# A difference made by GpSimd or by ScalarE: every second block of the modulated prompt rows in a streaming encoder layer

## The chip, the cores and the metric

The kernel runs on one core of a Trainium2 chip. A core has five engines that run their own instruction streams and wait for each other on semaphores: TensorE (PE: matrix products and transposes, results into PSUM), VectorE (DVE), ScalarE (ACT), GpSimd (POOL) and SyncE (SP, which issues most of the DMAs here). The on-chip memories are SBUF and PSUM; PSUM is used in eight banks of 128 x 512 fp32.

The metric is the device time of one execution in microseconds (us). Times below are medians of several executions; one further execution was recorded by the hardware profiler, and all lines of a profile or trace in this document come from such recorded executions.

## What is computed

The reference is one layer of a streaming encoder for a prompt of 2048 rows and for 8 running streams of 16 rows each, with rows of 1024 numbers. Its first step is a normalisation with a modulation per sequence:

```python
def adaln_modulate(x, c, norm_g, w_ada, b_ada):
    mod = c @ w_ada + b_ada
    shift, scale, gate = jnp.split(mod, 3, axis=-1)
    h = rms_norm(x, norm_g) * (1.0 + scale[:, None, :]) + shift[:, None, :]
    return h, gate[:, None, :]
```

From `h` follow ten projections (`h @ w_in`), rotary embedding of some of them, a differential attention with 4 heads, a stick-breaking attention with 8 heads, gates, a merge of the two branches, an output projection, a residual and a last normalisation. Keys and values are outputs too. All inputs and outputs are fp32.

## The kernel before

**Numbers.** TensorE is fed with fp16 pairs: a value v is kept as an upper half hi = fp16(v) and a lower half lo = fp16(v - hi), and a product of two such values takes three fp16 products (hi hi, hi lo, lo hi).

**Tiles.** The prompt has 16 tiles of 128 rows; the 8 streams together are a 17th tile, the sample tile. The rows are taken in five groups (`GROUPS`): groups 0 to 3 of 512 prompt rows (four tiles) and group 4, the sample tile.

**Phases.** In the first phase the conditioning vectors are multiplied with `w_ada` (`modulation`, six parts; parts 4 and 5, for the gate, run at the end of the phase), the rows are normalised (`normed`: squares on ScalarE at L298, a reciprocal root on VectorE at L258 to L269, then the scaling of the rows, for groups 1 to 3 by GpSimd at L1169, four instructions of 128 x 1024 for a group), and turned and modulated (`modulated`). The result h, as fp16 halves, goes to DRAM (`hT_d`), and the tiles in hand also feed projections directly. In the second phase eight units follow (unit = one pair of heads of one of the two attentions); each unit projects its 17 tiles (L467, gate products at L543), computes scores, weights and outputs. In the third phase the branches are merged and the output projection is made.

**`modulated(g)`, the place of the change.** One group is made in eight pieces k = 0 to 7, one for each 128 of the 1024 columns. A piece for a prompt group does this:

1. TensorE transposes four 128 x 128 fp32 blocks into one PSUM bank (L1233). Even k use a bank of the kind "s" (three of them), odd k a bank of the kind "o" (two of them).
2. ScalarE makes the upper half: hi = fp16(scale * p + shift), from PSUM into `hp` (L1239).
3. ScalarE makes hi - shift, fp32, into the scratch tile `tmp` (L1241); `minus_b` holds the negative shift, one number for each partition. `tmp` has two buffers, which `modulation` also uses (`ms`, L1144).
4. VectorE makes the lower half: lo = fp16(scale * p - tmp), from PSUM and `tmp` into `hp` (L1242). After it the bank and the scratch tile are free.
5. After the last piece SP stores the group (L1251).

The sample group (group 4) takes other lines (L1245 to L1249).

**Order.** Pieces of `modulated(g)`, of `normed(g + 1)` (or of the gate's modulation, for g = 3) and of the first projections of unit 0 (`take(position(...))`) are interleaved when the program is written down. The order on each engine is then set by a planner, which runs the program on a simulated time line (`schedule_with_timeline_sim=True`); instructions marked by `keep_in_program_order` keep theirs. On the chip each engine works through its stream in the planned order. In the profile the planner's order can be seen: upper halves run ahead of the differences of earlier pieces.

**Beside it.** Projections of unit 0 run in the same phase: TensorE's products (L467), ScalarE's scaled copy `pr` (L481), the upper halves of values, queries and keys (L318, L501), VectorE's lower halves of them (L323, L502), GpSimd's rotary embedding (L508, L510, L513) and SP's loads and stores.

Of the kernel before, what the change touches and what calls it, by code (L numbers as in the profile page):

```python
# [21 lines left out]
AF = mybir.ActivationFunctionType  # L22
ALU = mybir.AluOpType
# [101 lines left out]
def layer_kernel(ctx: ExitStack, tc: tile.TileContext, a: dict):  # L125
    nc = tc.nc
    V, S, G, T = nc.vector, nc.scalar, nc.gpsimd, nc.tensor
# [83 lines left out]
    def bank(tag, dt=F32):  # L211
        return ps.tile([P, 512 if dt == F32 else 1024], dt, tag=tag, name=f"ps_{tag}", bufs=BANKS[tag])
# [841 lines left out]
    with tc.tile_pool(name="p0", bufs=1) as p0:  # L1054
# [8 lines left out]
        def hp_tile(dt):  # L1063
            hp = p0.tile([P, 4096], F32, tag="hp", name="hp", bufs=3)
            return hp.bitcast(dt) if dt != F32 else hp
# [125 lines left out]
        def wide(x):  # L1191
# [24 lines left out]
                        scalar1=sh[:, 0:1], scalar2=None, op0=ALU.mult)  # L1216
        minus_b = p0.tile([P, KT], F32, name="minus_b")
        V.tensor_scalar(out=minus_b, in0=ab[:, 1, :, 0], scalar1=-1.0, scalar2=None, op0=ALU.mult)

        def modulated(g):  # L1220

            t0, w = GROUPS[g]
            nt = w // P
            box = {}

            def piece(k):
                if k == 0:
                    box["hp"] = hp = hp_tile(F16)[:, 0 : nt * 2 * D].rearrange("p (i a k n) -> p i a k n", a=2, k=KT, n=P)
                    at_hand.update({t0 // P + i: hp[:, i, :, :, :] for i in range(nt)})
                hp = box["hp"]  # L1230
                pt = bank("so"[k % 2])
                for i in range(nt):
                    T.transpose(pt[:, i * P : (i + 1) * P], xs[g][i][:, k * P : (k + 1) * P], ident)  # L1233
                tmp = p0.tile([P, 512], F32, tag="tmp", name="tmp", bufs=2)
                hi, lo = hp[:, :, 0, k, :], hp[:, :, 1, k, :]
                pv = pt[:, 0:w].rearrange("p (i n) -> p i n", n=P)
                tv = tmp[:, 0:w].rearrange("p (i n) -> p i n", n=P)
                if t0 < SEQ:
                    S.activation(out=hi, in_=pv, func=AF.Identity, scale=ab[:, 0, k, 0:1], bias=ab[:, 1, k, 0:1])  # L1239

                    S.activation(out=tv, in_=hi, func=AF.Identity, bias=minus_b[:, k : k + 1])  # L1241
                    V.scalar_tensor_tensor(out=lo, in0=pv, scalar=ab[:, 0, k, 0:1], in1=tv, op0=ALU.mult, op1=ALU.subtract)  # L1242
                else:
                    tb = tmp[:, 0:w].rearrange("p (b s) -> p b s", b=NB)
                    V.tensor_tensor(out=tb, in0=pt[:, 0:w].rearrange("p (b s) -> p b s", b=NB),  # L1245
                                    in1=ab[:, 0, k, 1:9].unsqueeze(2).to_broadcast([P, NB, NS]), op=ALU.mult)
                    V.tensor_tensor(out=tb, in0=tb, in1=ab[:, 1, k, 1:9].unsqueeze(2).to_broadcast([P, NB, NS]), op=ALU.add)
                    S.copy(out=hi, in_=tv)
                    G.tensor_tensor(out=lo, in0=tv, in1=hi, op=ALU.subtract)  # L1249
                if k == KT - 1:  # L1250
                    load(out=hT_d[g], in_=hp)  # L1251

            return [(1.0, lambda k=k: piece(k)) for k in range(KT)]

        def gates():
# [166 lines left out]
    for n in range(len(steps) + 2):  # L1422
# [19 lines left out]
        if at[0] == len(line) and not spare and not cached:  # L1442
            m = n - len(steps)
            if behind:
                k = -(-len(behind) * LATE_SHARE[m] // sum(LATE_SHARE[m:]))
                pieces += [(1.0, fn) for fn in behind[:k]]
                del behind[:k]
            if m >= -CUTS_AT:
                if cuts is None:
                    cuts = early_work()  # L1450
                k = -(-len(cuts) // (len(steps) + 2 - n))
# [189 lines left out]
```

## Time and profile before

| | us |
|---|---|
| median of 3 runs | 2224.91 |
| lowest and highest of them | 2220.69, 2227.12 |
| the profiled execution, whole time | 2226.87 |
| the profiled execution, span from the first to the last instruction | 2225.0 |

Durations are read from the profiled execution, so they are held against its own time; its whole time is 1.87 us above its span.

How to read the lines: an instruction is given by its line in the kernel, engine, operation, and out<-in by the names of the tiles with the shapes (partitions x elements, type). A group's line has its count, busy us and mean ns of one, and the idle time of the engine just before, with what ended it. A time line gives start, duration, and in brackets the idle time before, with its releaser. PEld are TensorE's weight loads, which overlap its products. A busy time in a stretch is the time in which an instruction of the engine was running; ends of products are modelled, since they are pipelined.

### The profile page before, as it was taken

What the parts mean: (1) busy time and instruction counts of PE and PEld (TensorE: products, weight loads), DVE (VectorE), ACT (ScalarE), POOL (GpSimd) and SP (SyncE); (2) the same over time, 40 slices, a digit from 0 to 9 for tenths busy, and PEclk for the clock granted to TensorE, in tenths of its full rate; (3) what the DMA queues carried; (4) which work ended last, traced back from release to release, by engine and by line L of the source; (5) the groups of instructions that cost most, each with busy time, mean ns of one, the idle gap of its engine ahead of it and who ended that gap; (6) DMA issues with size and microseconds to landing.
All of it is one profiled execution on the core that took longest, in us unless ns stands there. A gap on an engine that the chain in (4) does not pass through costs nothing.

```text
span 2225.0 us, 41210 instructions
## 1 busy us (share of the span) xinstructions
PE 2048.1 (92%) x14472; PEld 1089.3 (49%) x14472; DVE 1743.2 (78%) x3787; ACT 1605.3 (72%) x3212; POOL 719.5 (32%) x620
## 2 busy tenths in 40 slices
PE   3999999999999999999989998999997789899997
PEld 1545555555555455555554544555454344444443
DVE  5668868889886788988678888887689778787864
ACT  3978677788877787978777788876588575666531
POOL 0523024366311444742034365301345312211210
PEclk9999999999999999999999999999999899999999
DMA  9777669799796889979888999876677999889752
GB/s 333 261 246 183 128 151 224 181 221 209 184 266 164 217 199 207 212 192 227 190 207 203 182 237 223 231 171 136 151 165 174 192 280 251 217 250 235 188 155 67
DMA packets 824977, 451.03 MB, mean 203 GB/s; under 512 B 556122, under 2 KB 763274, under 8 KB 824256
## 3 DMA queue, kind: packets, MB, share of 16 engines
q1 hardware_dynamic: 823820, 448.01, 82.6%
q8 instruction: 113, 1.85, 0.4%
q14 instruction: 96, 0.79, 0.1%
q10 hardware_dynamic: 948, 0.39, 0.1%
HBM read 229.87 MB, written 86.02 MB: 142 GB/s over the span
## 4 chain that ended last, share of the span: by engine, by line
PE 27%; DVE 8%; DMA 7%; ACT 5%; issue 3%; POOL 2%; SPq 1%; DVEq 0%; POOLq 0%; ACTq 0%
PE ps_mm L467 7%; PE ps_t L543 6%; PE ps_o L1540 5%; PE ps_mm L1506 3%; DMA wt<-sc_n 2%; PE ps_s L708 1%; DVE sc_n L682 1%; PE ps_s L709 1%; DMA hs<-hT_d 1%; DMA hs<-o_d 1%; DMA dwt<-dsc 1%; ACT sc_p L134 1%; POOL sc_p L688 1%; PE ps_o L769 1%; ACT ps_s L134 1%
## 5 line engine op out<-in xcount | busy, mean ns | idle before, releaser
L688 POOL TENSOR_TENSOR sc_p<-sc_p,sc_n 128x127 f32<-128x127 f32 (+7 forms) x192 | 312.2, 1629 | 665.5 <-DVE sc_n L682 516.0
L467 PEld LDWEIGHTS <-hs 128*128 128x128 f16 x3120 | 293.3, 99 | 326.3 <-DMA hs<-hT_d 11.6
L467 PE MATMUL ps_mm<-wa,hs 128*128 128x512 f16 x1590 | 391.7, 382 | 10.8 <-DMA hs<-hT_d 9.2
L467 PE MATMUL ps_mm<-wb,hs 128*128 128x512 f16 x1530 | 380.1, 382 | 0.0
L682 DVE TENSOR_TENSOR_SCAN sc_n<-ps_s,sc_n,zero_t 128x512 f32<-128x512 f32 x192 | 245.4, 1278 | 30.6 <-ACT ps_s L134 25.1
L543 PE MATMUL ps_t<-wa,hs 128*128 128x512 f16 x1020 | 243.6, 381 | 3.3 <-DVE qst L576 2.3
L543 PEld LDWEIGHTS <-hs 128*128 128x128 f16 x1632 | 154.9, 98 | 186.2 <-DVE qst L576 6.3
L708 PE MATMUL ps_s<-k,qst 128*128 128x512 f16 (+3 forms) x640 | 222.8, 349 | 24.1 <-DVE sc_n L682 20.7
L619 DVE TENSOR_TENSOR sc_n<-sc_p,sc_n 128x128 f16<-128x128 f32 (+7 forms) x192 | 213.6, 1115 | 37.3 <-ACT sc_n L616 36.7
L134 ACT ACTIVATE sc_p<-ps_s,usc 128x512 f32<-128x512 f32 (+3 forms) x320 | 204.7, 640 | 36.0 <-PE ps_s L709 24.3
L709 PE MATMUL ps_s<-k,qst 128*128 128x512 f16 (+3 forms) x640 | 223.1, 349 | 0.0
L616 ACT CAST sc_n<-sc_p 128x128 f16<-128x128 f32 (+7 forms) x192 | 155.6, 811 | 60.6 <-POOL sc_p L688 59.9
L134 ACT ACTIVATE ps_s<-ps_s,usc 128x512 f32<-128x512 f32 (+3 forms) x320 | 197.0, 616 | 0.0
L543 PE MATMUL ps_t<-wb,hs 128*128 128x512 f16 x612 | 151.3, 382 | 7.8 <-DMA hs<-hT_d 4.4
L769 PE MATMUL ps_o<-v,wt 128*128 128x128 f16 x1088 | 134.4, 223 | 25.5 <-DMA wt<-sc_n 25.5
L1540 PE MATMUL ps_o<-wo,wb 128*128 128x512 f16 x624 | 144.8, 388 | 1.7 <-ACT wb L1314 1.7
L602 DVE TENSOR_SCALAR_CACHE_REDUCE sc_p<-ps_s,usc 128x512 f32<-128x512 f32 (+3 forms) x160 | 106.2, 664 | 33.3 <-PE ps_s L709 22.0
L1549 POOL TENSOR_TENSOR x<-m,x 128x512 f32<-128x512 f32 x32 | 47.0, 1468 | 255.4 <-DVE m L1544 161.8
L769 PEld LDWEIGHTS <-wt 128*128 128x128 f16 x1088 | 100.4, 100 | 54.3 <-DMA wt<-sc_n 29.6
L770 PE MATMUL ps_o<-v,wt 128*128 128x64 f16 x1088 | 126.2, 195 | 0.0
L682 DVE TENSOR_TENSOR_SCAN sc_n<-ps_s,zero_t 128x128 f32<-128x128 f32 (+3 forms) x128 | 104.1, 814 | 26.2 <-ACT ps_s L134 26.2
L1506 PEld LDWEIGHTS <-wa 128*128 128x128 f16 x816 | 77.8, 98 | 92.7 <-issue 6.3
(380 smaller groups left out, 4538.5 us busy)
## 6 DMA issues: line engine op xcount, KB each, us to landing
hs<-hT_d SPq DMA_DIRECT2D x132, 512.0 KB, 4.7
g_d<-gt SPq DMA_DIRECT2D x68, 256.0 KB, 4.7
out_dram<-pr SPq DMA_DIRECT2D x204, 64.0 KB, 3.3
o_d<-o SPq DMA_DIRECT2D x136, 64.0 KB, 2.3
wa<-g_d SPq DMA_DIRECT2D x17, 512.0 KB, 4.2
wb<-g_d SPq DMA_DIRECT2D x17, 512.0 KB
hs<-o_d SPq DMA_DIRECT2D x17, 512.0 KB, 4.0
wide<-in_w_ada_dram SPq DMA_DIRECT2D x8, 1024.0 KB, 12.6
```

The source lines that it names most:

```text
L134: i = S.activation(**kw)
L467: T.matmul(box["p"], box["h"][:, hi, k, :], U["w"][k][:, wi, :], start=(n == 0), stop=(n == 3 * KT - 1))
L543: x = T.matmul(box["g"][:, 0:gw], box["h"][:, hi, k, :], U["wg"][k // per][:, k % per, wi, :], start=(j == 0), stop=(j == 3 * KT - 1))
L616: x = S.copy(out=hi, in_=src)
L619: V.tensor_tensor(out=lo, in0=src, in1=hi, op=ALU.subtract)
L682: V.tensor_tensor_scan(out=dst[:, lo : lo + n][:, ::-1], data0=src[:, 0:n][:, ::-1], data1=zero_t[:, 0:1].to_broadcast([P, n]), initial=fi ...
L688: G.tensor_tensor(out=p[:, 0:m], in0=p[:, 0:m], in1=n[:, 1 : m + 1], op=ALU.mult)
L708: T.matmul(p[:, 0:n], qst[:, c, :], kk[:, c, 0:n], start=True, stop=False)
L709: T.matmul(p[:, 0:n], qst[:, 2 + c, :], kk[:, c, 0:n], start=False, stop=not diag)
L769: T.matmul(po[:, c * P : (c + 1) * P], wt[:, wj, :], vt[:, c, :, :], start=first, stop=False)
L1506: T.matmul(pb, st["u"][:, ui * 8 + br * 4 + k, :], wb[br * 4 + k // 2 * 2 + j][:, wi, k % 2, :], start=(n == 0), stop=(n == 11))
L1540: T.matmul(po, st["y"][:, yi * 8 + k, :], wo[j * 4 + k // 2][:, wi, k % 2, :], start=(n == 0), stop=(n == 3 * KT - 1))
```

## The change

For odd k (every second piece of groups 0 to 3) the difference hi - shift is made by a GpSimd instruction with two operations (add the negative shift, add zero), not by ScalarE's activation. Even k, the upper halves, the lower halves and the sample group stay as they are.

```diff
                 if t0 < SEQ:
                     S.activation(out=hi, in_=pv, func=AF.Identity, scale=ab[:, 0, k, 0:1], bias=ab[:, 1, k, 0:1])

-                    S.activation(out=tv, in_=hi, func=AF.Identity, bias=minus_b[:, k : k + 1])
+                    if k % 2:
+                        G.tensor_scalar(out=tv, in0=hi, scalar1=minus_b[:, k : k + 1], scalar2=0.0, op0=ALU.add, op1=ALU.add)
+                    else:
+                        S.activation(out=tv, in_=hi, func=AF.Identity, bias=minus_b[:, k : k + 1])
                     V.scalar_tensor_tensor(out=lo, in0=pv, scalar=ab[:, 0, k, 0:1], in1=tv, op0=ALU.mult, op1=ALU.subtract)
```

`G` is GpSimd, `S` ScalarE and `V` VectorE. The numbers written to `tv` are the same in both forms.

## The prediction

> **What bounds the kernel now.** I read the page's totals first, then the busy times of the stretch in which the changed line runs, then what each engine waited for there, and last the single instructions around those waits. The totals:
>
> ```profile
> span 2225.0 us, 41210 instructions
> PE 2048.1 (92%) x14472; PEld 1089.3 (49%) x14472; DVE 1743.2 (78%) x3787; ACT 1605.3 (72%) x3212; POOL 719.5 (32%) x620
> ```
>
> Over the whole span TensorE is the busiest engine; it is idle for 2225.0 - 2048.1 = 176.9 us. The changed line belongs to one short phase. The groups of ScalarE's instructions (line, operation, shapes, count, busy us, mean ns, idle before) and the busy times by stretch (stretch, length, then PE, PEld, DVE, ACT, POOL, granted clock, DMA) say how short:
>
> ```profile
> L1241 ACT ACTIVATE tmp<-hp,minus_b 128x512 f32<-128x512 f16 x32 | 22.3, 740 | 0.2
> 58.00:84.00 26.00, 21.96 (x132) 13.48 (x131) 18.48 (x50) 25.20 (x47) 17.07 (x20) 0.99 0.69 230
> 84.00:108.00 24.00, 23.42 (x157) 12.78 (x157) 12.44 (x24) 22.97 (x45) 8.49 (x12) 1.00 0.84 285
> 108.00:134.00 26.00, 23.77 (x169) 13.58 (x167) 13.44 (x34) 20.43 (x40) 6.54 (x9) 1.00 0.68 243
> sum 76.00, PE 69.16 PEld 39.83 DVE 44.36 ACT 68.60 POOL 32.10; mean PE 23.05 PEld 13.28 DVE 14.79 ACT 22.87 POOL 10.70
> ```
>
> All 32 instructions of the line lie in these 76 us. ScalarE is busy for 68.60 of them, TensorE for 69.16: two engines are full at once, because the planner fills TensorE with projection products of the first unit (L467) between the transposes. From 58 to 84 ScalarE has 0.80 us left. So relief of ScalarE can shorten this phase only where TensorE really stands still, 76.00 - 69.16 = 6.84 us in all. TensorE's waits there (waiter, released by, us in total, times, longest) name them:
>
> ```profile
> PE ps_s L1147 <- DVE col L307: 1.8, 1, 1.8
> PE ps_mm L467 <- ACT hp L1248: 1.7, 1, 1.7
> PE ps_o L1233 <- DVE hp L1242: 1.1, 1, 1.1
> PE ps_mm L467 <- POOL hp L1249: 1.1, 1, 1.1
> PE ps_mm L467 <- DVE v L323: 0.7, 1, 0.7
> PE ps_mm L1142 <- DVE v L323: 0.4, 1, 0.4
> ```
>
> They add up to 6.8 us. That is the ceiling of a direct gain, 0.31% of the span.
>
> **The change part by part.**
>
> Removed: 16 of the 32 differences leave ScalarE. Half of 22.3 us is 11.2 us busy, 68.60 becomes 57.4 of 76.
>
> Added: 16 GpSimd instructions, fp16 to fp32, 128x512, with two operations. The trace has no such form. The nearest rows are the weight halves of L320 (two operations, 128x512, fp32 to fp16, min/median/max ns) and, for an upper end, a 128x512 addition of two inputs:
>
> ```profile
> L320 POOL TENSOR_SCALAR wb<-wa,sw x4: 692/708/799, 138.5 to 140.6; 128x512 f16<-128x512 f32 x4
> L1549 POOL TENSOR_TENSOR x<-m,x 128x512 f32<-128x512 f32 x32 | 47.0, 1468 | 255.4 <-DVE m L1544 161.8 <-DVE usq L1357 48.8 <-DVE m L1547 27.8
> ```
>
> I take 0.71 us, since L320 has the size, the operation and one tensor input; the ends are 0.69 and 1.47 us. 16 x 0.71 = 11.4 us, and GpSimd goes from 32.10 to 43.5 us of 76 (at 1.47 us to 55.6). An odd block's difference therefore takes as long as before (0.71 against 0.74 us). A GpSimd result reaches a waiting engine quickly, and so does ScalarE's:
>
> ```profile
> 123.28 0.83 POOL L513 TENSOR_TENSOR rot<-rot,r 128x256 f32<-128x256 f32 x1
> 124.14 0.51 ACT L501 ACTIVATE qbuf<-rot,sq 128x256 f16<-128x256 f32 x1 [0.90 <-POOL rot L513]
> ```
>
> The addition ends at 124.11 and ScalarE starts at 124.14: a hop of 0.03 us, and the change adds one such hop to an odd block. I put it at nothing.
>
> Moved: nothing in DMA. The store of a group's h (L1251) is issued from SP after the last lower half as before; only GpSimd's queue has new entries.
>
> What the relief is worth at each wait, one by one. The 1.1 us of L1233 is a transpose of an odd block that waits for an odd bank, hence for VectorE's lower half, hence for the difference:
>
> ```profile
> 63.26 0.76 ACT L1239 ACTIVATE hp<-ps_o,ab 128x512 f16<-128x512 f32 x1
> ...
> 68.14 1.33 ACT L1241 ACTIVATE tmp<-hp,minus_b 128x512 f32<-128x512 f16 x2
> ...
> 68.89 0.75 DVE L1242 SCALAR_TENSOR_TENSOR hp<-ps_o,ab,tmp 128x512 f16<-128x512 f32 x1 [0.18 <-ACT tmp L1241]
> ```
>
> The upper half was there at 64.02, and ScalarE came to the difference only at 68.14. GpSimd can do it near 64, so I count the whole 1.1 us. The 1.8 us is VectorE's copy L1144 (the row names the instruction after it), which stood behind a lower half waiting for its difference:
>
> ```profile
> 120.12 0.75 DVE L1242 SCALAR_TENSOR_TENSOR hp<-ps_s,ab,tmp 128x512 f16<-128x512 f32 x1 [1.51 <-ACT tmp L1241]
> 120.97 0.69 DVE L1144 COPY tmp<-ps_mm 128x512 f32<-128x512 f32 x1
> ```
>
> That block is even (bank s) and keeps ScalarE; it profits only if ScalarE comes to it earlier. The 0.7 us waits for a value half behind ScalarE's full queue. I count half of these two, (1.8 + 0.7) / 2 = 1.25 us. The other three (1.7, 1.1, 0.4) stay: the first two are the sample tile's group, done on other lines, and the last a 0.4 us I leave. **Sum: 1.1 + 1.25 = 2.4 us** gained at the end of the phase, with 0 and 6.8 us as ends. Behind it TensorE stays the bound (379 of each 400 us, rows below), so I let the gain pass to the end.
>
> What VectorE could lose. While GpSimd runs, some VectorE instructions with both inputs in SBUF are stretched, the lower halves are not:
>
> ```profile
> 57.18 0.29 DVE L1247 TENSOR_TENSOR tmp<-tmp,ab 128x128 f32<-128x128 f32 x1
> ...
> 58.33 1.02 DVE L1247 TENSOR_TENSOR tmp<-tmp,ab 128x128 f32<-128x128 f32 x1
> ...
> 80.63 0.74 DVE L1242 SCALAR_TENSOR_TENSOR hp<-ps_s,ab,tmp 128x512 f16<-128x512 f32 x1
> ```
>
> The second L1247 starts inside a run of L1169 on GpSimd and takes 0.73 us more; the L1242 lies inside another such run and takes its usual 0.74. If each new instruction held up one VectorE instruction for its 0.71 us, that is at most 11.4 us, against 76.00 - 44.36 = 31.6 us that VectorE is free there. That cover is why I cost it at nothing; with no cover, a held-up instruction in front of a transpose would cost its 0.7 us. The Trainium skill, page "SBUF — State Buffer", section "Who interferes with whom", gives a rule that speaks against the change: GpSimd and VectorE share one pair of ports as an exclusive lock, taken by VectorE instructions with two SBUF inputs and by its two-port modes. By it the lower half, with one input in PSUM, is free of the lock and the sum stays; the trace agrees with 0.74 us inside the run.
>
> **The rivals.**
>
> ScalarE alone sets the pace (B). For it: 25.20 of 26 us at the start, no gap of note. Then all of TensorE's waits go, and the time falls by 6.8 us. Against it: three of the six waits do not hang on the moved instruction, and TensorE has only those 6.84 us to give. Time: 2218.1. The Trainium skill, "Perfetto Trace Analysis", section "Identifying the Most-Contended Engine", would judge for B: it takes occupancy for ScalarE and calls the busy share of matmuls a bad measure of headroom. The trace speaks against it in this phase: six L467 products follow each other every 0.216 us and leave no holes to close.
>
> ```profile
> 90.41 1.46 PE L467 MATMUL ps_mm<-wa,hp 128*128 128x512 f16 x6
> 91.71 0.28 PE L561 MATMUL ps_t<-id,k 128*128 128x128 f16 x2
> ```
>
> The slower side is GpSimd's queue (C). The differences stand in it behind runs of four L1169:
>
> ```profile
> 67.55 4.42 POOL L1169 TENSOR_SCALAR wide<-wide,rstd 128x1024 f32<-128x1024 f32 x4 [0.53 <-PE ps_mm L467]
> ...
> 78.26 4.42 POOL L1169 TENSOR_SCALAR wide<-wide,rstd 128x1024 f32<-128x1024 f32 x4 [4.09 <-issue]
> ```
>
> A difference caught behind a whole run is up to 4.4 us late. Queued behind the waiting lower half on VectorE are the next block's lower half and the value and key halves (L323), so products and transposes wait too. The slack is small: the next odd block's transposes take the bank some two us after the lower half ends,
>
> ```profile
> 79.96 0.75 DVE L1242 SCALAR_TENSOR_TENSOR hp<-ps_o,ab,tmp 128x512 f16<-128x512 f32 x1 [1.20 <-ACT tmp L1241]
> ...
> 82.86 0.60 PE L1233 MATMUL ps_o<-ident,wide 128*128 128x128 f32 x4
> ```
>
> 82.86 - 80.71 = 2.15 us. C decides when a difference is later than that: 4.4 - 2.15 = 2.3 us for each of the two runs, 4.6 us, and none of the gain: 2224.9 + 4.6 = 2229.5. At 1.47 us an instruction, two more 0.76 us, 2231. Against it: the planner knows both and can put differences between the four.
>
> The plan is drawn anew (D). The order of every engine is set by a simulated time line, and new durations early can shift choices to the end. Three stretches of like work show what layout is worth:
>
> ```profile
> 400.00:800.00 400.00, 382.08 (x2749) 209.71 (x2747) 334.89 (x707) 321.56 (x687) 155.22 (x134) 1.00 0.86 207
> 800.00:1200.00 400.00, 378.67 (x2705) 207.64 (x2703) 329.01 (x694) 316.43 (x673) 153.60 (x131) 0.99 0.88 204
> 1200.00:1600.00 400.00, 376.53 (x2654) 204.51 (x2652) 322.27 (x662) 309.16 (x662) 143.53 (x123) 0.98 0.85 193
> ```
>
> TensorE is idle 17.9, 21.3 and 23.5 us in them, a spread of 2.8. Some 5.2 such stretches follow the phase: 2.8 x the root of 5.2 = 6.4 us with mixed signs, 14.6 with one sign. I take 10 between them: 2212.5 (D down) or 2232.5 (D up). That the change does not do what it says is the 1.47 us end: GpSimd as slow as its two-input form; it goes with C.
>
> **How the numbers follow.** The sum is against the profiled execution: span 2225.0, 2226.87 us with what lies around it, which is 1.96 above the median of 2224.91. The forecast on the span is 2222.6, on the median 2224.9 - 2.4 = 2222.5, own range 2218 to 2225. About 0.3% (6.7 us, so 2218.2 and 2231.6) is what a measurement of this kernel can tell from no change. Chances: forecast 0.43, B 0.10, C 0.13, D down 0.16, D up 0.18. Faster takes D down and half of B, which ends on the bound: 0.21. Slower takes D up and a third of C: 0.22. Within: 0.57. Both signs of D are wanted in the range, with a few us of spread each: 2211 to 2235.
>
> **What would show it.** In the changed profile ScalarE's 58 to 134 us should read near 57 us, L1241 x16, a new GpSimd group x16 near 710 ns, and TensorE's wait for L1242 near 64 to 70 us gone. Idle of TensorE before L1233 released by L1242, with GpSimd's L1169 ahead of it, is C. An unchanged start of the units and another idle sum after 134 us is D. An instruction far from 0.71 us, a phase shorter by more than 6.8 us, or lower halves stretched beside GpSimd would make the prediction wrong.

## The result and the profile after

The changed kernel takes 2241.47 us (median of 6, 2235.26 to 2242.55), the kernel before 2223.28 us (6, 2220.69 to 2230.45): a ratio of 1.0082, 95% interval 1.0065 to 1.0099. It is slower by 18.2 us where 2222.5 was forecast, and beyond the range's end of 2235. In the kernel after, the lines behind L1241 are shifted: **L1242** is GpSimd's difference for odd k, **L1244** ScalarE's for even k, **L1245** the lower half (L1242 before), **L1254** the store of a group (L1251 before), L1251 and L1252 the sample group's. L1233, L1239 and everything ahead of L1241 keep their numbers.

The totals of the kernel after, from the page:

```profile
span 2239.7 us, 41224 instructions
PE 2057.5 (92%) x14472; PEld 1095.9 (49%) x14472; DVE 1753.2 (78%) x3787; ACT 1597.9 (71%) x3196; POOL 745.3 (33%) x636
```

TensorE executes the same 14472 products; by the page its idle time grew from 176.9 to 182.2 us and its busy time by 9.4 us, to which we come back under the clock. The first place to look is the phase. The kernel after, busy times by stretch (columns as in the prediction):

```profile
58.00:84.00 26.00, 17.07 (x85) 8.69 (x84) 19.68 (x48) 17.98 (x33) 22.92 (x23) 0.93 0.47 141
84.00:108.00 24.00, 23.27 (x148) 13.36 (x147) 10.21 (x20) 18.78 (x35) 18.37 (x16) 1.00 0.72 246
108.00:134.00 26.00, 23.32 (x159) 13.15 (x158) 13.40 (x27) 19.48 (x36) 17.52 (x15) 0.93 0.83 314
sum 76.00, PE 63.66 PEld 35.20 DVE 43.29 ACT 56.25 POOL 58.81; mean PE 21.22 PEld 11.73 DVE 14.43 ACT 18.75 POOL 19.60
```

ScalarE fell to 56.25 us (57.4 was worked out; some of the phase's work now lies behind 134 us). GpSimd rose to 58.81, not to 43.5; in the first stretch it is busy for 22.92 of 26 us and TensorE for 17.07, where it had 21.96. The line itself says why. The kernel after, one line's instructions (min/median/max ns, first and last start us):

```profile
L1242 POOL TENSOR_SCALAR tmp<-hp,minus_b x16: 1997/1998/2037, 67.5 to 135.3; 128x512 f32<-128x512 f16 x16
```

**One instruction takes 2.00 us, not 0.71**, and all sixteen do. The stores of h, the same view before and then after:

```profile
L1251 SPq DMA_DIRECT2D hT_d<-hp x5: 320/339/605, 67.1 to 133.3; - x5
```

```profile
L1254 SPq DMA_DIRECT2D hT_d<-hp x5: 319/343/414, 67.5 to 142.7; - x5
```

The last group is stored at 142.7 instead of 133.3: the phase ends 9.4 us later. Its first upper half (L1239) starts at 59.2 us after and at 58.8 before, so 9.0 us of this arise in the phase itself. What TensorE waited for from 58 to 134 us after the change (waiter, releaser, us in total, times, longest):

```profile
PE ps_o L1233 <- DVE hp L1245: 6.1, 2, 4.2
PE ps_s L1233 <- DVE hp L1245: 1.9, 2, 1.1
PE ps_mm L467 <- POOL hp L1252: 1.8, 1, 1.8
PE ps_mm L467 <- ACT hp L1251: 1.7, 1, 1.7
```

Transposes wait 8.0 us for a bank that a lower half has to free; before, 1.1 us. How the longest of these comes about shows in the time line of the kernel after (GpSimd's rows, with those of the other engines that belong to the chain):

```profile
67.55 2.00 POOL L1242 TENSOR_SCALAR tmp<-hp,minus_b 128x512 f32<-128x512 f16 x1
67.89 0.77 ACT L1239 ACTIVATE hp<-ps_o,ab 128x512 f16<-128x512 f32 x1
69.52 4.41 POOL L1169 TENSOR_SCALAR wide<-wide,rstd 128x1024 f32<-128x1024 f32 x4
73.89 0.73 POOL L508 TENSOR_TENSOR rot<-pr,rope 128x256 f32<-128x256 f32 x1
73.96 0.68 DVE L262 TENSOR_SCALAR rstd<-rs_i 128x4 int32<-128x4 int32 x1 [0.99 <-POOL wide L1169]
74.57 0.73 POOL L510 TENSOR_TENSOR r<-pr,rope 128x256 f32<-128x256 f32 x1
75.28 3.97 POOL L1242 TENSOR_SCALAR tmp<-hp,minus_b 128x512 f32<-128x512 f16 x2
78.58 0.16 DVE L269 TENSOR_TENSOR rstd<-rstd,rs_t 128x4 f32<-128x4 f32 x1
78.66 0.75 DVE L1245 SCALAR_TENSOR_TENSOR hp<-ps_o,ab,tmp 128x512 f16<-128x512 f32 x1
79.47 0.66 PE L1233 MATMUL ps_o<-ident,wa 128*128 128x128 f32 x4 [4.16 <-DVE hp L1245]
79.51 0.72 ACT L1244 ACTIVATE tmp<-hp,minus_b 128x512 f32<-128x512 f16 x1 [3.38 <-DVE hp L1245]
```

The upper half of an odd block is there at 68.66. Its difference stands behind the four L1169, L508 and L510, and starts at 75.28; with 2.00 us for itself it ends at 77.28. VectorE reaches the lower half at 78.66, after the reciprocal roots of the next group (L262 to L269), which stood as one block from 73.96. TensorE's transposes then start at 79.47 after 4.16 us of idle time, and ScalarE, which was to be relieved, stands still for 3.38 us behind the same lower half, since `tmp` has only two buffers. In this order the 2.00 us are not the last thing on the path: an instruction of 0.70 us would have ended at 75.98, and the lower half would still have stood behind the roots until 78.58. The longest wait is made by the places in the two streams as well as by the instruction's time.

The wait has an echo on TensorE itself. The kernel after, its products before and behind the wait, and the stretches around it (the last three columns are the granted clock, the DMA share and GB/s):

```profile
72.12 2.75 PE L467 MATMUL ps_mm<-wa,hp 128*128 128x512 f16 x12
...
79.96 4.44 PE L467 MATMUL ps_mm<-wa,hp 128*128 128x512 f16 x12
```

```profile
80.00:82.00 2.00, 2.00 (x9) 0.77 (x7) 1.74 (x3) 1.86 (x5) 2.00 (x2) 0.64 0.45 121
82.00:84.00 2.00, 2.00 (x6) 0.70 (x5) 2.00 (x3) 0.49 (x1) 2.00 (x3) 0.51 0.96 265
84.00:86.00 2.00, 2.00 (x15) 1.42 (x14) 0.07 (x1) 1.12 (x2) 2.00 (x2) 1.00 0.60 171
```

Twelve products of the same form take 2.75 us before the idle time of 4.16 us and 4.44 behind it, at a granted clock near one half: the wait costs 1.7 us more than its own length, and this time counts as busy. The Trainium skill, page "TensorE: Matmul & The Clock Gate", section "What's actually happening", says that the clock is halved after an idle window of about 3.4 us and restored after about as long of work. In this trace the clock reads one half from 80.5 to 84.0 us, which agrees with the second part; on the first part the traces do not agree if one wait is meant. The kernel after has a second such stretch, from 121.5 to 124.9 us, behind a wait of 1.97 us, and in e5_fast below it is one from 88.7 to 92.1 us behind a wait of 1.78 us.

The rest comes later. The start of the n-th TensorE product, counted from 0 in order of time, against the n-th of the kernel before (worked out from the traces; positive is late; the plans order products differently, so it is not always the same one) shows where the profiled execution falls behind; the columns of four experiments are used below:

| product n | before, us | after | e2 | e4 | e5 | e7 |
|---|---|---|---|---|---|---|
| 800 | 165.6 | 10.4 | -6.3 | 2.4 | 0.6 | -1.3 |
| 1200 | 225.9 | 15.1 | -10.1 | 8.8 | -2.6 | -4.2 |
| 2400 | 401.5 | 14.2 | -11.4 | 8.4 | -4.4 | -6.4 |
| 6400 | 984.7 | 20.5 | -8.2 | 9.3 | -2.2 | -7.1 |
| 12800 | 1952.5 | 15.6 | -1.0 | -3.6 | -6.6 | -12.4 |
| 14471, the last | 2213.9 | 15.0 | -3.2 | -4.5 | -7.9 | -12.1 |

About 10 us are lost by 166 us, another 5 by 226 us, and from there it wavers around 15 to 20. (The profiled execution of before lies 3.6 us above its own median, so its column is that much too long at the end; that of e2 lies 3.4 us above its own, those of e4, e5 and e7 lie 6.3, 4.5 and 2.9 us below theirs.)

How much of such a difference means something can be read from two runs described below, e1_forms and e9_pairs. They add instructions at the very end only, and all their 14472 products stand in the order of the kernel before. Against it they are 2.6 and 2.1 us late at product 800, 2.3 and 2.4 at 1200, 0.4 and 0.8 at 2400, 1.9 and 3.5 at 6400, and 4.1 and 8.7 early at the last one. So 2 to 4 us up to product 6400, and up to 9 at the end, come without any change of the order; most of the 2 us at the start lie ahead of the phase already.

The second loss has a wait of its own. The kernel after, TensorE's waits from 150 to 275 us, and the time line around the second of them:

```profile
PE ps_o L765 <- DMA wt<-sc_n: 4.4, 2, 2.5
PE ps_mm L467 <- DVE qbuf L502: 3.5, 1, 3.5
```

```profile
237.01 1.81 DVE L657 SCALAR_TENSOR_TENSOR sc_p<-sc_n,r,sc_p 128x1024 f32<-128x1024 f32 x2
238.74 1.68 DVE L323 SCALAR_TENSOR_TENSOR sc_n<-sc_p,r,sc_n 128x1024 f16<-128x1024 f32 x2
240.33 0.35 DVE L502 SCALAR_TENSOR_TENSOR qbuf<-ps_mm,usc,qbuf 128x128 f16<-128x128 f32 x1
240.73 1.23 PE L467 MATMUL ps_mm<-wb,hs 128*128 128x512 f16 x3 [3.50 <-DVE qbuf L502]
```

The 0.35 us L502 that frees a PSUM bank stands behind 3.4 us of attention weights in VectorE's stream; the kernel before has no such wait there. TensorE's clock is at one half behind this wait too, from 241.0 to 244.4 us. In the kernel before it is never halved between 58.5 and 543 us.

### The profile page after: what moved, and what is told of

Read it like the earlier page. It is cut to its first block, busy times and chain, and to the rows that moved or that the text cites. A ratio compares the mean times of both kernels' runs of the same rounds, so it can differ in the third digit from the quotient of the medians.

```text
span 2239.7 us, 41224 instructions
## 1 busy us (share of the span) xinstructions
PE 2057.5 (92%) x14472; PEld 1095.9 (49%) x14472; DVE 1753.2 (78%) x3787; ACT 1597.9 (71%) x3196; POOL 745.3 (33%) x636
## 4 chain that ended last, share of the span: by engine, by line
PE 49%; DVE 17%; DMA 13%; ACT 9%; issue 6%; POOL 3%; SPq 2%; DVEq 0%; POOLq 0%; ACTq 0%
PE ps_mm L467 18%; PE ps_t L543 10%; PE ps_o L1543 4%; DMA wt<-sc_n 4%; DVE sc_n L682 4%; PE ps_s L708 3%; PE ps_s L709 3%; PE ps_mm L1509 3%; DMA hs<-o_d 2%; ACT sc_p L134 2%; POOL sc_p L688 1%; DVE sc_n L619 1%; PE ps_o L769 1%; ACT ps_s L134 1%; ACT sc_n L616 1%
## 5 line engine op out<-in xcount | busy, mean ns | idle before, releaser
L619 DVE TENSOR_TENSOR sc_n<-sc_p,sc_n 128x128 f16<-128x128 f32 (+7 forms) x192 | 218.8, 1143 | 33.0 <-ACT sc_n L616 32.4
L602 DVE TENSOR_SCALAR_CACHE_REDUCE sc_n<-ps_s,usc 128x512 f32<-128x512 f32 (+3 forms) x160 | 106.1, 663 | 23.6 <-PE ps_s L709 14.2
```

The costliest lines, as they stand in the source:

```text
L602: V.tensor_scalar(out=dst[:, lo : lo + n], in0=p[:, 0:n], scalar1=sc_pos, scalar2=None, op0=ALU.mult, op1=ALU.max, accum_out=job["mx"][:, ...
L619: V.tensor_tensor(out=lo, in0=src, in1=hi, op=ALU.subtract)
```

## The experiments

The theory after the result: the 2.00 us of GpSimd's instruction, on the path through the odd banks, makes the phase late (**G**). Rivals: the queue behind L1169 does it whatever the instruction takes (**Q**), or the new plan does (**D**). And it was open why the instruction takes 2.00 us. All times below are medians against the kernel before on the same chip, with the 95% interval of the ratio. Edits are shown against the kernel after, those of e1_forms and e9_pairs against the kernel before.

The phase starts at a somewhat different time in each recorded execution, so its length is the better measure: from the start of the first upper half (L1239) to the last store of h.

| | first upper half, us | last store of h, us | length of the phase, us | against before |
|---|---|---|---|---|
| before | 58.8 | 133.3 | 74.5 | |
| e1_forms, phase unchanged | 61.4 | 135.9 | 74.5 | 0.0 |
| e9_pairs, phase unchanged | 60.9 | 135.4 | 74.5 | 0.0 |
| after | 59.2 | 142.7 | 83.5 | 9.0 longer |
| e2_dve | 58.3 | 128.2 | 69.9 | 4.6 shorter |
| e3_quarter | 60.4 | 141.8 | 81.5 | 7.0 longer |
| e4_late | 60.5 | 134.0 | 73.5 | 1.0 shorter |
| e5_fast | 60.3 | 133.5 | 73.2 | 1.4 shorter |
| e6_fast_even | 60.6 | 133.0 | 72.4 | 2.1 shorter |
| e7_fast_late | 60.6 | 131.5 | 70.9 | 3.6 shorter |
| e8_null | 60.6 | 135.8 | 75.2 | 0.7 longer |
| e10_mix | 59.5 | 129.6 | 70.1 | 4.5 shorter |
| e11_late_all | 59.9 | 129.7 | 69.8 | 4.7 shorter |

Three executions of the unchanged phase agree within 0.1 us in this length.

**e1_forms.** The kernel before (no change in the phase) with pairs of instructions added at its end, on GpSimd and on VectorE, in each form that could matter: rows of 128 or contiguous, fp16 or fp32, two pairs of operations.

```diff
...
+        for E in (G, V):
+            for out, src, o1 in ((w4, s16, ALU.add), (w32, c16, ALU.add), (w32, c16, ALU.mult), (w32, a32, ALU.add), (w4, s32, ALU.add),
+                                 (w16, a32, ALU.mult), (w16, c16, ALU.add), (w32[:, 0:256], c16[:, 0:256], ALU.add)):
+                for _ in range(2):
+                    E.tensor_scalar(out=out, in0=src, scalar1=one, scalar2=0.0, op0=o1, op1=ALU.add)
...
```

> The kernel before, with 22 small GpSimd and 22 small VectorE instructions added at its very end, two of each form, where the other engines are idle (nothing of the layer is left out). What is read is the duration of each form at 128x512. Theory A (the fp16 input makes GpSimd slow): every GpSimd form with an fp16 input and one fp32 output takes about 2.0 us, laid out in rows or not and whatever the operation, the half-width one about 1.0 to 1.1 us, and the forms with fp32 input 0.5 to 0.8 us. Rival B (the rows of 128 with gaps make it slow): 2.0 us in the two forms with gaps alone, 0.7 us in the others. Rival C (VectorE holds GpSimd up at the place of the change): all one-input forms about 0.7 us here. VectorE's forms: 0.3 to 0.8 us in all theories.

Measured on GpSimd, 128x512, the two of each in ns: (add, add) fp16 rows to fp32 2012 and 1999; contiguous 2010 and 2125; fp32 input 1997 and 2540, in rows 2300 and 1998; fp16 to fp16 1997 and 1999. **(mult, add) fp16 to fp32: 697 and 696**; fp32 to fp16 1152 and 695. At 128x256 (add, add) takes 1144 twice. A copy takes 611 and 612, an addition of two tensors 1157 to 1262. Two rows from the time line of e1_forms: the (add, add) form of the change, and one of (mult, add) with the same input and output types:

```profile
2200.20 2.01 POOL L1627 TENSOR_SCALAR wa<-wb,ones 128x512 f32<-128x512 f16 x1 [1.23 <-DVE wb L1619]
...
2213.67 0.70 POOL L1627 TENSOR_SCALAR wa<-wb,ones 128x512 f32<-128x512 f16 x1
```

Both print alike: the profile does not show the operations. Neither the input's type nor its rows nor another engine makes it slow; the pair of operations does. None of the three theories of the expectation had that. The single longer ones (2540, 2300, 2125, 1152) are not explained.

**e2_dve.** Odd differences on VectorE. The phase is relieved of ScalarE's work without GpSimd.

```diff
-                        G.tensor_scalar(out=tv, in0=hi, scalar1=minus_b[:, k : k + 1], scalar2=0.0, op0=ALU.add, op1=ALU.add)
+                        V.tensor_scalar(out=tv, in0=hi, scalar1=minus_b[:, k : k + 1], scalar2=None, op0=ALU.add)
```

> The difference of odd blocks is made by VectorE, neither ScalarE nor GpSimd. Theory A (the loss comes from 2.0 us a block on GpSimd and its queue): VectorE's instruction takes 0.4 to 0.75 us, VectorE is busy for some 52 of the phase's 76 us, the last group of h is stored within 3 us of the kernel before (133.3 us), and the time is 2217 to 2230 us. Rival P (it is the plan drawn anew that costs, whoever makes the difference): 2233 us or more here too, although the phase ends on time.

2219.92 us, ratio 0.9994 (0.9979 to 1.0008): no difference that can be told. Its line:

```profile
L1242 DVE TENSOR_SCALAR tmp<-hp,minus_b x16: 477/486/1018, 66.6 to 125.7; 128x512 f32<-128x512 f16 x16
```

The phase is 4.6 us shorter, and the lead is 11.4 us at 400 us of the profiled execution, but 1.0 to 3.2 at the end, where the runs with the unchanged order are 4.1 and 8.7 us early. What relief of ScalarE can gain is there in the phase, and is given back before the end; what takes it back was not looked for.

**e3_quarter and e4_late.** Half of the slow instructions each: `k = 3, 7` of all groups, or odd k of groups 2 and 3 only, which lie behind the runs of L1169.

```diff
-                    if k % 2:
+                    if k % 4 == 3:
```

```diff
-                    if k % 2:
+                    if k % 2 and g > 1:
```

> GpSimd makes the difference in every fourth block only (k = 3 and 7), 8 instructions and not 16. Theory A: the last group of h is stored 2 to 6 us later than before, not 9.4, and the time is 2226 to 2234 us. Rival P: no proportion to the number of instructions; the time can be 2241 us or 2223 us with the phase's end as A says.

> GpSimd makes the difference of odd blocks in groups 2 and 3 only, 8 instructions, all behind the runs of L1169. Theory A with the queue behind L1169 as the larger part: the phase ends 0 to 4 us later than before, and the time is 2223 to 2230 us. Theory A with the 2.0 us alone (each block costs alike): phase 4 to 5 us later, 2230 to 2234 us. Rival P: the order of the instructions behind the phase is nearly that of the changed kernel here, so what the changed kernel loses behind the phase (5 to 8 us) is lost here too: 2230 to 2236 us with a phase that ends on time.

e3_quarter 2235.59, ratio 1.0056 (1.0036 to 1.0076); e4_late 2228.37, 1.0028 (1.0013 to 1.0042). Both have eight instructions of 1.996 us. The stores of h, e3_quarter and then e4_late:

```profile
L1254 SPq DMA_DIRECT2D hT_d<-hp x5: 320/343/522, 68.6 to 141.8; - x5
```

```profile
L1254 SPq DMA_DIRECT2D hT_d<-hp x5: 319/374/456, 68.9 to 134.0; - x5
```

Eight of them spread over all groups make the phase 7.0 us longer, eight behind the runs of L1169 leave it 1.0 us shorter: the place counts more than the number. And e4_late is slower than before although its phase is not longer. It loses 6.4 us between products 800 and 1200 (table above), like the kernel after, with the same wait in that stretch (143 to 268 us):

```profile
PE ps_mm L467 <- DVE qbuf L502: 2.6, 1, 2.6
```

TensorE's clock is at one half there from 201.8 to 205.2 and from 229.1 to 239.4 us.

**e5_fast.** The change with the operations exchanged: multiply by one, add the negative shift. The same numbers are written, in the same place, by the same engine.

```diff
-                        G.tensor_scalar(out=tv, in0=hi, scalar1=minus_b[:, k : k + 1], scalar2=0.0, op0=ALU.add, op1=ALU.add)
+                        G.tensor_scalar(out=tv, in0=hi, scalar1=1.0, scalar2=minus_b[:, k : k + 1], op0=ALU.mult, op1=ALU.add)
```

> The change with another pair of operations in the GpSimd instruction: times 1, plus the negative shift, where the changed kernel adds the negative shift and then 0. The numbers written are the same. Theory A2 (the pair add, add is dear on GpSimd, 2.0 us; multiply, add costs 0.70 us; place and queue are harmless): L1242 takes 0.70 us, the last group of h is stored at 126 to 134 us (133.3 before, 142.7 changed), and the time is 2215 to 2227 us. Rival Q (the queue behind the runs of L1169 makes the phase late, whatever one instruction takes): the last store stays at 138 us or later, 2232 us or more. Rival P (the redrawn plan): stored on time, but 2229 us or more.

2223.05 us (12 runs), ratio 1.0000 (0.9986 to 1.0014). The new line, the stores, and the sum of the busy times from 58 to 134 us, e5_fast:

```profile
L1242 POOL TENSOR_SCALAR tmp<-hp,minus_b x16: 693/695/697, 68.7 to 128.4; 128x512 f32<-128x512 f16 x16
```

```profile
L1254 SPq DMA_DIRECT2D hT_d<-hp x5: 319/339/456, 68.8 to 133.5; - x5
```

```profile
sum 76.00, PE 69.59 PEld 40.03 DVE 46.20 ACT 60.43 POOL 42.78; mean PE 23.20 PEld 13.34 DVE 15.40 ACT 20.14 POOL 14.26
```

The instruction takes 0.695 us, the phase is 1.4 us shorter than before, GpSimd is busy for 42.78 us where 43.5 was worked out. The queue is still there, as the time line of e5_fast and its waits from 58 to 134 us show:

```profile
69.50 4.41 POOL L1169 TENSOR_SCALAR wide<-wide,rstd 128x1024 f32<-128x1024 f32 x4
73.90 0.69 POOL L1242 TENSOR_SCALAR tmp<-hp,minus_b 128x512 f32<-128x512 f16 x1
```

```profile
PE ps_o L1233 <- DVE hp L1245: 3.2, 3, 1.8
PE ps_mm L467 <- POOL hp L1252: 1.8, 1, 1.8
```

Transposes wait 3.2 us for lower halves, against 8.0 in the kernel after and 1.1 before. So with the short form, and the plan that is drawn for it, all 9.0 us of the phase are gone and 1.4 more, where 2.4 had been forecast; Q as forecast (138 us or later, 2232 us or more) is refuted, though some 2 us of waits for lower halves remain. How much of the 9.0 us is the instruction's time and how much the order is not shown: the plans differ (here the difference stands directly behind the L1169, and the lower half ahead of the rest of the roots, at 75.90), and exchanging the operations under an unchanged plan was not tried. The wait for L502 behind the phase is absent here, and so is the second loss.

**e6_fast_even, e7_fast_late, e11_late_all, e10_mix.** The short form in other places: even k; odd k of groups 2 and 3; all k of groups 2 and 3; and odd k on VectorE in groups 0 and 1, on GpSimd in 2 and 3.

```diff
-                    if k % 2:
+                    if k % 2 == 0:
```

```diff
-                    if k % 2:
+                    if k % 2 and g > 1:
```

```diff
-                    if k % 2:
+                    if g > 1:
```

```diff
-                    if k % 2:
+                    if k % 2 and g > 1:
+                        G.tensor_scalar(out=tv, in0=hi, scalar1=1.0, scalar2=minus_b[:, k : k + 1], op0=ALU.mult, op1=ALU.add)
+                    elif k % 2:
+                        V.tensor_scalar(out=tv, in0=hi, scalar1=minus_b[:, k : k + 1], scalar2=None, op0=ALU.add)
```

> The same short GpSimd instruction, for even blocks (banks s, of which there are three) and not for odd ones (banks o, two). Theory A2: as with odd blocks, last store at 126 to 134 us, 2215 to 2227 us. Rival P: the work is the same as for odd blocks, but the plan is another, so the time may differ from that of the odd blocks by 5 us or more.

> The short GpSimd instruction for odd blocks of groups 2 and 3 only, 8 instructions; against the run with 2.0 us in the same places (2228.4 us) it changes the pair of operations alone. Theory A2: last store at 128 to 133 us, 2217 to 2227 us. Rival P: 2229 us or more with a phase that ends on time.

> The short GpSimd instruction for all blocks, odd and even, of groups 2 and 3: 16 instructions. Theory A2: GpSimd has room there (12.4 us busy of 50 in the kernel before), last store at 126 to 132 us, 2213 to 2223 us. If GpSimd's two banks in a row make the lower halves late: last store at 133 us or later, 2222 us or more.

> The difference of odd blocks by VectorE in groups 0 and 1 and by the short GpSimd instruction in groups 2 and 3; ScalarE keeps the even blocks. If the relief of ScalarE adds up and the runs of L1169 are avoided: last store at 124 to 130 us, and 2211 to 2219 us, below the 2217.3 us of groups 2 and 3 alone. Rival P: the phase is shorter and the lead is given back later, 2217 to 2224 us.

| | us | ratio (95%) | last store of h, us |
|---|---|---|---|
| e6_fast_even | 2225.30 | 1.0015 (1.0001 to 1.0029) | 133.0 |
| e7_fast_late | 2217.27 | 0.9975 (0.9961 to 0.9988) | 131.5 |
| e11_late_all | 2222.88 | 1.0008 (0.9995 to 1.0021) | 129.7 |
| e10_mix | 2224.85 | 1.0015 (1.0001 to 1.0028) | 129.6 |

e7_fast_late beats both kernels, by 0.25% against before. It also forms a pair with e4_late, with the same eight places and other operations: 2228.37 against 2217.27. But the phase's length does not put these four in order of time: in e10_mix and e11_late_all the phase is 4.5 and 4.7 us shorter, and they are not faster. So e7_fast_late's gain cannot be put down to the phase; of its 12 us lead in the profiled execution 1.3 us are there at product 800, and the unchanged order shows up to 8.7 us at the end. No run varied the order at the same phase. Part of it may be a lucky plan, picked out of several.

**e8_null.** No GpSimd: odd differences stay on ScalarE, in a form with another operand, so that the plan is drawn anew while the work stays.

```diff
-                        G.tensor_scalar(out=tv, in0=hi, scalar1=minus_b[:, k : k + 1], scalar2=0.0, op0=ALU.add, op1=ALU.add)
+                        S.activation(out=tv, in_=hi, func=AF.Identity, scale=ones[:, 0:1], bias=minus_b[:, k : k + 1])
```

> The kernel before, with the difference of odd blocks still on ScalarE, written with a scale of 1 read from SBUF: the same work on the same engines, but a plan that is drawn anew (some of the order of every engine differs). Theory A2: ScalarE's instruction takes 0.74 us, the phase ends as before, and the time is within 4 us of before. Rival P (a redrawn plan is worth 5 us and more by itself): a difference of 5 us or more in either direction.

2222.68 us, ratio 1.0003 (0.9990 to 1.0015). A new plan by itself need cost nothing; but this one is nearer to the old than the others (at 351 of the 14472 places in TensorE's order stands another product than before, at 1217 in the kernel after). The probe is not quite null:

```profile
L1242 ACT ACTIVATE tmp<-hp,minus_b,ones x16: 810/836/922, 69.9 to 134.2; 128x512 f32<-128x512 f16 x16
```

0.836 us instead of 0.740: 16 x 0.1 us more on ScalarE, in the phase where it is fullest, makes the phase 0.7 us longer. In the whole time that is within the interval, so it decides nothing about rival B.

**e9_pairs.** The kernel before with ten forms of GpSimd's instruction at its end, fp16 to fp32, 128x512, two of each.

```diff
...
+        for s1, o0, s2, o1 in ((one, ALU.add, None, None), (one, ALU.subtract, None, None), (one, ALU.mult, None, None), (1.0, ALU.add, None, None),
+                               (1.0, ALU.mult, one, ALU.add), (one, ALU.mult, one, ALU.mult), (one, ALU.mult, one, ALU.subtract),
+                               (one, ALU.add, 1.0, ALU.mult), (1.0, ALU.add, 0.0, ALU.add), (one, ALU.max, 0.0, ALU.add)):
+            for _ in range(2):
+                kw = {} if o1 is None else dict(op1=o1)
+                G.tensor_scalar(out=w32, in0=c16, scalar1=s1, scalar2=s2, op0=o0, **kw)
```

> The kernel before with 20 GpSimd instructions of 128x512, fp16 to fp32, added at its end, two of each of ten forms of operations (nothing of the layer is left out). Theory A2 (only the pair multiply, add has a short way on GpSimd): multiply by 1 and add a value read from SBUF 0.70 us, single operations 0.6 to 0.75 us, every other pair 1.9 to 2.2 us. Rival R (it is the first operation: multiply is short, add is long): multiply, multiply and multiply, subtract 0.70 us, and all that begin with add, subtract or maximum, single ones too, about 2.0 us.

The two of (add, mult), and the two of (max, add), from the time line of e9_pairs:

```profile
2220.84 1.47 POOL L1623 TENSOR_SCALAR wa<-wb,ones 128x512 f32<-128x512 f16 x2
...
2226.44 4.09 POOL L1623 TENSOR_SCALAR wa<-wb,ones 128x512 f32<-128x512 f16 x2
```

In ns, in the order written: add alone 1575 and 1562, subtract alone 1567 and 2076, multiply alone 1567 and 1929, add a constant alone 1492 and 2150; (mult, add) 1009 and 984, (mult, mult) 771 and 767, (mult, subtract) 2082 and 2072, **(add, mult) 686 and 686**, (add, add) of constants 1937 and 1922, (max, add) 1997 and 1992. The later ones of the single operations and (mult, add) lie beside other work at the kernel's end, so their spread is not read; (mult, add) is 0.695 in e5_fast. One operation alone takes 1.49 us or more, and only the three pairs made of multiplications, or of one with an addition, come under 1.1. Neither theory of the expectation fits: (mult, add) is not the only short pair, and (mult, subtract) is long though it begins with a multiplication. Dropping the second addition would not have saved the change.

## Why the prediction was wrong, step by step

**What bounds the phase: right.** Two full engines, and TensorE's own 6.8 us of idle time as the ceiling. e2_dve, which relieves ScalarE without GpSimd, made the phase 4.6 us shorter, within that ceiling. For rival B, by which all 6.8 us go, that is too little, and in the whole time nothing of it is left.

**Removed: right.** ScalarE at 57.4 of 76 us was worked out, 56.25 measured, though the later phase takes part in that: in e5_fast it is 60.43, since other work moves in.

**Added: this step failed.** "I take 0.71 us, since L320 has the size, the operation and one tensor input; the ends are 0.69 and 1.47 us." L320 multiplies and adds zero; the change adds and adds zero. The row's name is the same (TENSOR_SCALAR), the operations are not, and the profile prints no operations: they stood in the code at L320. The instruction took 1.998 us, above even the upper end, so the term 16 x 0.71 = 11.4 us was 32.0. The size and the one input had been taken for what matters, and the upper end was another instruction (an addition of two tensors) where a slower one-input form was not thought of. With (mult, add) the same edit takes 0.695 us, close to the forecast term, and 2223.05 us in all, a ratio of 1.0000 (0.9986 to 1.0014), in which the forecast gain of 2.4 us (a ratio of 0.9989) cannot be told from none. The Trainium skill, page "GPSIMD Engine Reference", section "Elementwise — side-by-side cycle accounting", puts the some 2.6 cycles an element of an addition of two tensors down to its two inputs, and gives about 1.8 as the best case of a loop. Here one input with two additions takes 2.00 us and two inputs 1.16 to 1.26 us, so an order by the number of inputs alone does not hold.

**Rival C: the right place at the wrong price.** The queue behind L1169, the odd bank, the lower half and the products behind it are what the trace shows. Its price of 4.6 to 6 us was built from a difference of 0.71 to 1.47 us; with 2.00 us transposes wait 8.0 us and the phase is 9.0 us longer. It stays with 0.695 us too (3.2 us of waits in e5_fast). The planner did not put differences between the four L1169, which had been counted against C. What it put instead made it worse: the whole block of reciprocal roots stood ahead of the lower half.

**Stretched VectorE work at nothing: right for the lower halves.** The kernel after, beside GpSimd's instructions, lower halves and reciprocal roots:

```profile
L1245 DVE SCALAR_TENSOR_TENSOR hp<-ps_o,ab,tmp x16: 739/742/751, 70.4 to 142.0; 128x512 f16<-128x512 f32 x16
```

```profile
75.35 0.62 DVE L267 TENSOR_TENSOR rs_t<-rs_t,rs_q 128x4 f32<-128x4 f32 x1
...
76.61 0.16 DVE L267 TENSOR_TENSOR rs_t<-rs_t,rs_q 128x4 f32<-128x4 f32 x1
76.80 0.49 DVE L268 TENSOR_SCALAR rs_t<-rs_t 128x4 f32<-128x4 f32 x1
...
78.18 0.16 DVE L267 TENSOR_TENSOR rs_t<-rs_t,rs_q 128x4 f32<-128x4 f32 x1
```

The lower halves keep their 0.74 us, with one input in PSUM, as the rule of the Trainium skill, page "SBUF — State Buffer", section "Who interferes with whom", has it. The 128x4 instructions fit that rule only in part. All four above lie inside GpSimd's two differences from 75.28 to 79.25 us: L267, with two SBUF inputs, is held up at the start of the first (0.62) and not later in it or in the second (0.16), and L268, with one, is held up once (0.49). Summed over the root's lines from 58 to 143 us, the excess over 0.16 us is 4.5 us after and 3.0 before, but 4.4 in e5_fast too, whose phase is not longer: this is not where the time went.

**The gain passes to the end: wrong in its general form.** e2_dve's lead of 11.4 us shrinks to 3.2 in its profiled execution, less than the unchanged order's 4.1 and 8.7, and the medians differ by 2.4 us, within the interval. The kernel after is 10.4 us late at product 800 and 15.0 at the last: its delay was not given back.

**Rival D: partly true.** Some 5 us of the loss arise between 166 and 226 us, behind the phase, where VectorE's order puts attention weights ahead of L502. e4_late has that loss and that wait with a phase that is not longer; e5_fast, e7_fast_late and e8_null have neither. So it goes with the order of these plans and not with the phase's length. That the order alone makes it is argued, not shown: no run held one fixed and varied the other. D's size of 10 us was too large: the new plans without the slow instruction (e2, e5, e6, e7, e8, e10, e11) lie between -0.25% and +0.15% of before, -5.6 to +3.3 us.

Added up: 9.0 us of the phase, gone with the short form and its plan, and about 5 behind it, against 15.0 at the end of the profiled executions. The medians lie 18.2 us apart, since the profiled execution of before was 3.6 us above its median. Where these last 3 to 4 us arise is open: against the two runs of the unchanged order the kernel after loses another 3.6 to 4.8 us between products 2400 and 6400.

**Not in the sum at all: the clock.** Behind the wait of 4.16 us TensorE's clock was halved for 3.4 us. The prediction added waits as their own lengths; this one cost 1.7 us more. It is not small here: between 58.5 and 400 us the kernel after has three such stretches (from 80.5, 121.5 and 241.0 us) and the kernel before none. By estimate that is 3 x 1.7 = 5.1 us, part of the two losses above. From 58 us to the end TensorE is busy at half clock for 74.0 us after and 60.7 before, which by the same halving makes, by estimate, 6.7 of the 9.4 us by which its busy time grew. Yet e5_fast has such stretches too, one of them shown here, and its phase is not longer:

```profile
90.00:92.00 2.00, 2.00 (x7) 0.63 (x6) 1.29 (x2) 1.57 (x4) 2.00 (x3) 0.50 0.74 186
```

## What to carry to other kernels

Price a GpSimd instruction by a row whose operations are the same in the code, not by a row of the same name and shape; if there is none, leave the upper end open, or write the operation so that a priced pair does it (here a multiplication by one and an addition, at a third of the time). An engine with free time can still be the wrong place: what counts is what stands ahead of the new instruction in its stream, and which scarce buffer waits behind it. And with a planner that redraws everything, a difference of five us between versions of one edit may come from orders far behind the place of the edit; recorded executions of one and the same order show how much of it comes without any change.

## What the runs showed of the hardware beyond this

In these runs GpSimd's tensor_scalar on 128x512 takes 0.69 to 0.77 us for (mult, add), (add, mult) and (mult, mult), 1.9 to 2.1 us for (add, add), (max, add) and (mult, subtract), and 1.49 us or more for one operation alone, apart from the longer ones named above; for (add, add) type and layout make no difference, and on 256 columns it takes 1.144 us, so by estimate about 3.3 ns a column ((1999 - 1144) / 256) on some 0.3 us. Why the operations decide is not known from these runs. On VectorE (add, add) and (mult, add), the two pairs tried there, take 0.485 to 0.488 us on 128x512 once GpSimd's added instructions are done, and three of the four beside them 0.62 to 0.91. ScalarE's activation with its scale read from SBUF takes 0.836 us against 0.740 with none.
